# One-hots of the G build stored token by token in a hybrid SSM / attention / PEER kernel

## The chip, the cores and the metric

The kernel runs on one core of one Trainium2 chip. The metric is the device time of one execution in microseconds (us), the median of several runs. TensorE is PE in the rows (PEld is its weight load), VectorE is DVE, ScalarE is ACT, GpSimd is POOL, and SP issues DMAs.

## The reference

A residual stream of 512 tokens by 1024 runs through one Mamba-2 layer and one sliding-window attention layer, and behind each of them through a PEER feed-forward layer and a gated embedding. Only PEER matters here:

```python
q = (h @ q_w).reshape(T, PEER_HEADS, 2, PEER_HALF)
s = jnp.einsum('thcd,ckd->thck', q, sub_keys)            # 8 heads x 2 halves x 128 keys
s1, i1 = lax.top_k(s[:, :, 0], 16)
s2, i2 = lax.top_k(s[:, :, 1], 16)
cand_s = s1[..., :, None] + s2[..., None, :]             # 256 candidates per head
cand_i = i1[..., :, None] * 128 + i2[..., None, :]
best_s, best_pos = lax.top_k(cand_s, 16)
idx  = take_along_axis(cand_i, best_pos)                 # 8 x 16 experts of 16384 per token
gate = softmax(best_s)
a = einsum('nd,nhkd->nhk', h, u[idx]);  w = gate * gelu(a)
out = einsum('nhk,nhkd->nd', w, v[idx])
```

## The kernel before, in words

The 128 tokens of the first token tile (tt = 0) are done as the reference says: their 128 expert rows each are gathered by indirect DMA (lines 678 to 695). For the other 384 tokens (ND) the kernel computes all 16384 experts densely, in 128 blocks of 128 experts, and multiplies by a matrix G that holds the gate of each chosen expert and zero elsewhere.

The function `peer(L)` runs once for each of the two layers. Its first part makes queries, scores and the first top-k. Its u loop then runs over 128 blocks: each block is 24 float32r matmuls of 384 columns in `lin` / `mm3` (lines 202 to 204), the weights of which come by DMA, are split into a high and a low half on ScalarE (line 169) and GpSimd (line 172, four pieces), and the result goes through Gelu to DRAM (line 990). Beside it a generator `bg()` is advanced: `self.step(BRATE)` hands out 2.65 units of credit per block, and each item of its list has a cost (6.0 a top-k, 5.0 half a decode, 1.5 a one-hot batch). Beside that again, 1.17 gathers per block run (`gather(URATE)`). The v loop follows with 24 matmuls per block and no G work.

The G items are what the change touches. One item is a batch of QT = 4 tokens; there are 96 a layer, 192 in all. For a batch, `onehot(b)` on VectorE makes two tiles of 1024 fp16 elements per partition (a partition is one of the 128 head-and-rank slots): `o` (line 880; its tile shares the name "early" with score tiles), which compares the numbers 0 to 127 (`iota`) with both halves of the expert index (`iT`), and `og` (line 882), which multiplies the first half's one-hot by the gate's high and low fp16 part (`gT`). One item later `gmm(b, o)` issues 8 fp16 matmuls of 128x128 by 128 columns (line 895, for each of 4 tokens two that add up in one PSUM bank), and ScalarE copies the bank out (line 896) into a tile from which G goes to DRAM. A group of 8 such matmuls is called a burst below. The one-hot of the next item is made while a burst runs: `o` has three buffers, `og` two, so VectorE waits at line 882 when it is two bursts ahead.

In memory the token is the innermost dimension before: `o` is [2 halves, 128 numbers, 4 tokens], so that the four tokens of one number lie side by side, VectorE reads the indices of four tokens as a run of four fp16, and a matmul reads one token's one-hot with a step of 4 elements (8 bytes):

```python
mm(ps[:, q * P:(q + 1) * P], o[0][:, 1, :, q], o[1][:, j, :, q], start=(j == 0), stop=(j == 1))
```

`o[0][:, 1, :, q]` is the stationary operand (weight load), `o[1][:, j, :, q]` the moving one. `iT` and `gT` are filled in `decode_e`'s `turn` from a PSUM transpose (lines 868 to 870), three times a layer. The decode (lines 831 to 838) also reads the first 16 entries of `iota`, each four times side by side.

Of the kernel before, what the change touches and what calls it, by code (L numbers as in the profile page):

```python
# [16 lines left out]
AF = _mybir.ActivationFunctionType  # L17
OP = _mybir.AluOpType
AX = _mybir.AxisListType

P = 128
# [5 lines left out]
TOPK = 16  # L27
NBLK = 128
NG = P
ND = NT - NG  # L30
# [4 lines left out]
QT = 4  # L35
GSCALE = 32768.0
F16 = _mybir.dt.float16
# [11 lines left out]
C_ID, C_TRI, C_ROT, C_IOTA, C_I16, C_INV = 0, 128, 256, 384, 512, 528  # L49
# [13 lines left out]
class Net:  # L63
# [54 lines left out]
    def plan(self):  # L118
        t, s = self.t, self.srcs
        w, off = t["wlin"], 0  # L120

        def lin(n):
            nonlocal off
            for _ in range(n):
                s.append(w[off])
                off += 1

        def peer(i):
            lin(16)
            for j in range(NBLK):  # L130
                s.append(t["ut"][i * NBLK + j])
            for j in range(NBLK):
                s.append(t["v"][i * NBLK + j])

        lin(66)
        peer(0)
        lin(8 + 21)
        peer(1)
        lin(8)
# [500 lines left out]
    def peer(self, L):  # L640
        nc, t, tc = self.nc, self.t, self.tc
        mm = nc.tensor.matmul
        vt = nc.vector
# [103 lines left out]
        with ExitStack() as ctx:  # L747
            mp = ctx.enter_context(tc.tile_pool(name="pm", bufs=2, reuse_waits="tile"))
            hp = ctx.enter_context(tc.tile_pool(name="ph", bufs=1, reuse_waits="tile"))
# [24 lines left out]
            early = {}  # L774
            best = hp.tile([P, NTT, HEADS, TOPK], F32, name="best")
            pos = hp.tile([P, NTT, HEADS, TOPK], U32, name="pos")
            idx = hp.tile([P, 2, NTT, HEADS, TOPK], U32, name="idx")
            iT = hp.tile([P, 2, ND], F16, name="iT")
            gT = hp.tile([P, 2, ND], F16, name="gT")
            iota = hp.tile([P, P, QT], F16, name="iota")  # L780
            vt.tensor_copy(iota, self.const[:, C_IOTA:C_IOTA + P, None].to_broadcast([P, P, QT]))

            def top16(items):
                for f in (lambda x, v, i: vt.max(v[:, 0:8], x),
# [23 lines left out]
            HK = HEADS * TOPK  # L808
            dec = {}

            def fl(ap):
                return ap.rearrange("p a b -> p (a b)")
# [7 lines left out]
            def decode_i(tt, c):  # L820
                pi = mp.tile([P, HEADS, TOPK], U32, name="pi", bufs=1)
                if c == 0:
                    vt.tensor_single_scalar(pi, pos[:, tt], 4, op=OP.logical_shift_right)
                else:
                    vt.tensor_single_scalar(pi, pos[:, tt], 15, op=OP.bitwise_and)
                pb = mp.tile([P, TOPK, HEADS], F16, name="pb", bufs=1)
                vt.tensor_copy(pb, pi.rearrange("p h k -> p k h"))
                ib = mp.tile([P, TOPK, HEADS], F16, name="ib")
                vt.tensor_copy(ib, idx[:, c, tt].rearrange("p h a -> p a h"))
                eq = mp.tile([P, TOPK, HK], F16, name="eq", bufs=1)  # L830
                vt.tensor_tensor(eq.rearrange("p a (n q) -> p a n q", q=QT),  # L831
                                 fl(pb).rearrange("p (n q) -> p n q", q=QT)[:, None].to_broadcast([P, TOPK, HK // QT, QT]),
                                 iota[:, :TOPK, None, :].to_broadcast([P, TOPK, HK // QT, QT]), op=OP.is_equal)
                e4 = eq.rearrange("p a (k h) -> p a k h", h=HEADS)
                vt.tensor_tensor(e4, e4, ib[:, :, None, :].to_broadcast([P, TOPK, TOPK, HEADS]), op=OP.mult)  # L835
                n = TOPK // 2
                while n > 1:
                    vt.tensor_tensor(eq[:, :n], eq[:, :n], eq[:, n:2 * n], op=OP.add)  # L838
                    n //= 2
                f = mp.tile([P, HK], F32, name=f"fi{c}", bufs=1)  # L840
                vt.tensor_tensor(f, eq[:, 0], eq[:, 1], op=OP.add)
                dec[tt][1].append(f)

            def decode_e(tt):
                gt, fi = dec.pop(tt)
                sm = mp.tile([P, 2, HEADS], F32, name="sm")
                vt.tensor_reduce(sm[:, 0], gt, axis=AX.X, op=OP.add)
                vt.reciprocal(sm[:, 1], sm[:, 0])
                gk = mp.tile([P, TOPK, HEADS], F32, name="gk", bufs=1)
                vt.tensor_tensor(gk, gt.rearrange("p h k -> p k h"), sm[:, 1, None, :].to_broadcast([P, TOPK, HEADS]),  # L850
                                 op=OP.mult)
                if tt == 0:
                    ef = wg[:, 0]
                    vt.tensor_scalar(ef, fi[0], float(P), float(L * NBLK * P), op0=OP.mult, op1=OP.add)
                    vt.tensor_tensor(ef, ef, fi[1], op=OP.add)
                    vt.tensor_copy(eg, ef)
                    vt.tensor_copy(gate, fl(gk))

                def turn():
                    if tt == 0:  # L860
                        self.gi = 0
                        return
                    pt = self.bank(7)
                    for j, src in enumerate(fi + [fl(gk)]):
                        nc.tensor.transpose(pt[:, j * P:(j + 1) * P], src, self.ident)
                    ts = slice(tt * P - NG, (tt + 1) * P - NG)
                    for j in range(2):
                        nc.scalar.activation(iT[:, j, ts], pt[:, j * P:(j + 1) * P], AF.Copy)
                    nc.scalar.activation(gT[:, 0, ts], pt[:, 2 * P:3 * P], AF.Copy, scale=GSCALE)
                    vt.scalar_tensor_tensor(gT[:, 1, ts], pt[:, 2 * P:3 * P], GSCALE, gT[:, 0, ts], op0=OP.mult,  # L870
                                            op1=OP.subtract)
                return turn

            gs = {}

            def onehot(b):
                o = mp.tile([P, 2, P, QT], F16, name="early", bufs=3)
                og = mp.tile([P, 2, P, QT], F16, name="og")
                ts = slice(QT * b - NG, QT * b - NG + QT)
                vt.tensor_tensor(o, iota[:, None].to_broadcast([P, 2, P, QT]),  # L880
                                 iT[:, :, None, ts].to_broadcast([P, 2, P, QT]), op=OP.is_equal)
                vt.tensor_tensor(og, o[:, 0:1].to_broadcast([P, 2, P, QT]), gT[:, :, None, ts].to_broadcast([P, 2, P, QT]),  # L882
                                 op=OP.mult)
                return o, og

            def gmm(b, o):
                b -= NG // 4
                if b % GQ == 0:
                    i = b // GQ % 2
                    gs[b // GQ] = gsz[0][:, 4 * i:4 * i + 4].rearrange("p a b -> p (a b)").rearrange("p (a t) -> p a t", t=GT)  # L890
                x = gs[b // GQ]
                ps = gb()
                for q in range(4):
                    for j in range(2):
                        mm(ps[:, q * P:(q + 1) * P], o[0][:, 1, :, q], o[1][:, j, :, q], start=(j == 0), stop=(j == 1))  # L895
                nc.scalar.activation(x.rearrange("p a t -> p t a")[:, 4 * (b % GQ):4 * (b % GQ) + 4, :],
                                     ps.rearrange("p (q a) -> p q a", q=4), AF.Copy, scale=1.0 / GSCALE)
                if b % GQ == GQ - 1:
                    nc.scalar.dma_start(G[b // GQ], x.rearrange("p a t -> p (a t)"))
# [9 lines left out]
            def bg():  # L909
# [6 lines left out]
                def D(tt):  # L916
                    items.append((0.3, lambda: decode_g(tt), 2))
                    items.append((5.0, lambda: decode_i(tt, 0)))
                    items.append((5.0, lambda: decode_i(tt, 1)))
                    items.append((0.8, lambda: decode_e(tt), 2))  # L920

                def G_(tt, lo, hi):
                    def one(b):
                        o = onehot(b)
                        return lambda: gmm(b, o)
                    for b in range(32 * tt + lo, 32 * tt + hi):
                        items.append((1.5, lambda b=b: one(b)))
# [24 lines left out]
            for c in range(2 * HEADS):  # L952
                if c < 2:
                    ps = pair[c]
                else:
                    ps = mmb()
# [5 lines left out]
                q = hp.tile([P, NT], F32, name="ga", bufs=3)  # L962
# [16 lines left out]
            for j in range(NBLK):  # L979
                ps = mmb()  # L980
# [22 lines left out]
        with vctx:  # L1003
            mp = vctx.enter_context(tc.tile_pool(name="pv", bufs=3, reuse_waits="tile"))
# [549 lines left out]
```

## Time and profile before

| | us |
|---|---|
| median of 3 runs | 3490.18 (3489.79 to 3500.37) |
| the profiled execution | 3494.42 |
| its span in the trace | 3492.6 |
| u loop with G items, layer 0 | about 700 to 1210 |
| u loop with G items, layer 1 | about 2280 to 2793 |

TensorE is busy in 97% of the span, VectorE in 76%, GpSimd in 56%, ScalarE in 42%. Matmuls are pipelined and their recorded durations overlap, so how much time one takes is read from the distance between two starts, not from its duration. [...]

### The profile page before, as it was taken

The page shows a single profiled execution, that of the slowest core. Times are in us where ns is not written, and L with a number is a line of the kernel's source. Part 1 is how long each engine was busy: PE and PEld are TensorE (multiplying, and loading weights), DVE is VectorE, ACT ScalarE, POOL GpSimd, SP SyncE. Part 2 cuts the span into 40 slices and gives each one's busy share as a digit, 9 for nine tenths or more (in the row PEclk, how much of TensorE's full clock was granted, in tenths as well). Part 3 has the DMA queues.
Part 4 walks back from the last instruction along what each step waited for, and adds up shares of the span by engine and source line. Part 5 has one row for each costly group of instructions (what it writes and reads, how often), then busy time and mean ns, then how long its engine had stood idle before and what let it go on. Part 6 is the DMA issues. An engine that isn't in the chain of part 4 may idle for free.

```text
span 3492.6 us, 52247 instructions
## 1 busy us (share of the span) xinstructions
PE 3374.0 (97%) x18814; PEld 3109.2 (89%) x18814; DVE 2647.7 (76%) x4878; ACT 1454.1 (42%) x2198; POOL 1941.5 (56%) x2168
## 2 busy tenths in 40 slices
PE   8999999999999999999998999999999999999997
PEld 6777777999999989999996668999999999999996
DVE  7666677898888637887777956899888637877775
ACT  4443333444445533333334553444445533333334
POOL 5445445788887882322216235788888784222214
PEclk9999999999999999999999999999999999999998
DMA  3222222588888889999983122488888889999982
GB/s 119 89 72 73 73 67 69 166 295 283 312 303 288 309 292 365 349 341 347 338 281 107 43 67 87 148 274 299 299 317 281 301 309 357 349 342 336 341 306 85
DMA packets 357300, 827.50 MB, mean 237 GB/s; under 512 B 30000, under 2 KB 196528, under 8 KB 350896
## 3 DMA queue, kind: packets, MB, share of 16 engines
q1 hardware_dynamic: 235136, 448.59, 39.2%
q0 software_dynamic: 73728, 268.47, 21.3%
q10 hardware_dynamic: 48176, 107.10, 8.0%
q8 instruction: 147, 2.41, 0.3%
q14 instruction: 113, 0.93, 0.1%
HBM read 717.09 MB, written 106.95 MB: 236 GB/s over the span
## 4 chain that ended last, share of the span: by engine, by line
PE 70%; DVE 18%; POOL 5%; DMA 3%; issue 3%; ACT 1%; SPq 0%; POOLq 0%; ACTq 0%; DVEq 0%
PE bank L202 20%; PE bank L203 20%; PE bank L204 20%; PE bank L895 4%; POOL wlo L172 3%; DVE row L678 2%; DMA row<-u,eg 2%; DVE eq L838 1%; DVE og L882 1%; DVE early L880 1%; POOL row L695 1%; PE bank L968 1%; DVE eq L835 1%; PE bank L542 1%; DVE eq L831 1%
## 5 line engine op out<-in xcount | busy, mean ns | idle before, releaser
L172 POOL TENSOR_TENSOR wlo<-wraw,whi 128x256 fp32r<-128x256 f32 x1564 | 1262.3, 839 | 601.0 <-ACT whi L169 553.0
L169 ACT ACTIVATE whi<-wraw 128x1024 fp32r<-128x1024 f32 x647 | 685.3, 1061 | 760.3 <-issue 303.5
L204 PE MATMUL bank<-hhi,wlo 128*128 128x384 f32 x2048 | 697.2, 340 | 14.0 <-POOL wlo L172 13.9
L202 PE MATMUL bank<-hhi,whi 128*128 128x384 f32 x2048 | 707.8, 346 | 0.4 <-ACT whi L169 0.4
L695 POOL DMA_INDIRECT row<-v,eg x256 | 294.2, 1149 | 733.5 <-DVE yg L687 719.0
L203 PE MATMUL bank<-hlo,whi 128*128 128x384 f32 x2048 | 695.7, 340 | 0.0
L203 PE MATMUL bank<-vlo,whi 128*128 128x384 f32 x2032 | 684.2, 337 | 6.4 <-DVE vlo L744 6.4
L202 PE MATMUL bank<-vhi,whi 128*128 128x384 f32 x2032 | 684.8, 337 | 0.8 <-ACT vhi L742 0.8
L204 PE MATMUL bank<-vhi,wlo 128*128 128x384 f32 x2032 | 683.7, 336 | 0.0
L172 DVE TENSOR_TENSOR wlo<-wraw,whi 128x1024 fp32r<-128x1024 f32 x256 | 313.1, 1223 | 148.6 <-ACT whi L169 147.3
L204 PEld LDWEIGHTS bank<-hhi,wlo 128*128 128x128 f32 x2048 | 387.4, 189 | 19.8 <-POOL wlo L172 19.4
L202 PEld LDWEIGHTS bank<-hhi,whi 128*128 128x128 f32 x2048 | 390.2, 191 | 0.8 <-ACT whi L169 0.8
L203 PEld LDWEIGHTS bank<-vlo,whi 128*128 128x128 f32 x2032 | 382.6, 188 | 8.2 <-DVE vlo L744 8.2
L203 PEld LDWEIGHTS bank<-hlo,whi 128*128 128x128 f32 x2048 | 388.9, 190 | 0.0
L202 PEld LDWEIGHTS bank<-vhi,whi 128*128 128x128 f32 x2032 | 382.7, 188 | 2.0 <-ACT vhi L742 1.5
L204 PEld LDWEIGHTS bank<-vhi,wlo 128*128 128x128 f32 x2032 | 382.6, 188 | 0.1
L678 DVE SCALAR_TENSOR_TENSOR row<-row,pair 128x1024 f32<-128x1024 f32 x256 | 305.5, 1211 | 96.1 <-DMA row<-u,eg 96.1
L687 DVE SCALAR_TENSOR_TENSOR yg<-row,wg,yg 128x1024 f32<-128x1024 f32 x254 | 327.9, 1291 | 38.0 <-DMA row<-v,eg 38.0
L202 PE MATMUL bank<-z,whi 128*128 128x512 f32 x728 | 320.2, 440 | 3.4 <-DVE sg L1134 3.4
L990 ACT ACTIVATE ga<-bank 128x384 f32<-128x384 f32 x256 | 125.6, 491 | 471.1 <-PE bank L204 470.8
L695 POOL DMA_INDIRECT row<-u,eg x256 | 276.1, 1079 | 49.6 <-issue 23.4
L203 PE MATMUL bank<-z,whi 128*128 128x512 f32 x728 | 291.1, 400 | 4.7 <-DVE z L262 4.7
(321 smaller groups left out, 4995.9 us busy)
## 6 DMA issues: line engine op xcount, KB each, us to landing
wraw<-ut SPq DMA_DIRECT2D x256, 512.0 KB, 4.5
wraw<-v SPq DMA_DIRECT2D x256, 512.0 KB, 6.1
wraw<-wlin SPq DMA_DIRECT2D x135, 512.0 KB, 3.4
GA<-ga ACTq DMA_DIRECT2D x256, 192.0 KB, 4.2
G<-gsz ACTq DMA_DIRECT2D x48, 1024.0 KB, 7.0
gv<-G SPq DMA_DIRECT2D x96, 512.0 KB, 9.5
gsz<-GA SPq DMA_DIRECT2D x256, 192.0 KB, 6.8
PJ<-nf ACTq DMA_DIRECT2D x16, 256.0 KB, 2.0
```

The lines of the kernel that those rows point to most:

```text
L169: nc.scalar.activation(hi, r, AF.Copy)
L172: self.lo_eng.tensor_tensor(lo[:, q:q + n], r[:, q:q + n], hi.bitcast(F32)[:, q:q + n], op=OP.subtract)
L202: mm(out, whi, xhi, start=start, stop=False)
L203: mm(out, whi, xlo, start=False, stop=False)
L204: mm(out, wlo, xhi, start=False, stop=stop)
L542: mm(o[r * 64:(r + 1) * 64], X[:, (2 * q + r) * 64:(2 * q + r + 1) * 64], M[:, 2 * q + r, :], start=(c == 0), stop=True, skip_group_check= ...
L678: vt.scalar_tensor_tensor(r, r, 1.0, self.pair, op0=OP.mult, op1=OP.mult, accum_out=wg[:, 0, j:j + 1])
L687: vt.scalar_tensor_tensor(yg, r, wg[:, 0, j:j + 1], yg, op0=OP.mult, op1=OP.add)
L695: nc.gpsimd.indirect_dma_start(out=got[i], out_offset=None, in_=t["u"] if i < NJ else t["v"].rearrange("a p d -> (a p) d"), in_offset=bass ...
L831: vt.tensor_tensor(eq.rearrange("p a (n q) -> p a n q", q=QT), fl(pb).rearrange("p (n q) -> p n q", q=QT)[:, None].to_broadcast([P, TOPK, ...
L895: mm(ps[:, q * P:(q + 1) * P], o[0][:, 1, :, q], o[1][:, j, :, q], start=(j == 0), stop=(j == 1))
L990: nc.scalar.activation(ga[:, NG:], ps[:, NG:], AF.Gelu)
```

## The change

The tiles of the one-hots become [4 tokens, 2 halves, 128 numbers]: each token's 128 fp16 lie side by side, for the weight load as for the moving operand. The index and gate tiles get a last dimension of 2 that holds the same value twice, so that VectorE's operand, which is now the same for all 128 numbers of a token and half, is read as a pair of equal fp16, 64 times over. `iota` is no longer stored four times; a small tile `i16` takes its place in the decode.

```diff
-            iT = hp.tile([P, 2, ND], F16, name="iT")
-            gT = hp.tile([P, 2, ND], F16, name="gT")
-            iota = hp.tile([P, P, QT], F16, name="iota")
-            vt.tensor_copy(iota, self.const[:, C_IOTA:C_IOTA + P, None].to_broadcast([P, P, QT]))
+            iT = hp.tile([P, ND, 2, 2], F16, name="iT")
+            gT = hp.tile([P, ND, 2, 2], F16, name="gT")
+            iota = hp.tile([P, P], F16, name="iota")
+            vt.tensor_copy(iota, self.const[:, C_IOTA:C_IOTA + P])
+            i16 = hp.tile([P, TOPK, QT], F16, name="i16")
+            vt.tensor_copy(i16, self.const[:, C_I16:C_I16 + TOPK, None].to_broadcast([P, TOPK, QT]))
...
-                                 iota[:, :TOPK, None, :].to_broadcast([P, TOPK, HK // QT, QT]), op=OP.is_equal)
+                                 i16[:, :, None, :].to_broadcast([P, TOPK, HK // QT, QT]), op=OP.is_equal)
...
+                    two = lambda j: pt[:, j * P:(j + 1) * P, None].to_broadcast([P, P, 2])
                     for j in range(2):
-                        nc.scalar.activation(iT[:, j, ts], pt[:, j * P:(j + 1) * P], AF.Copy)
-                    nc.scalar.activation(gT[:, 0, ts], pt[:, 2 * P:3 * P], AF.Copy, scale=GSCALE)
-                    vt.scalar_tensor_tensor(gT[:, 1, ts], pt[:, 2 * P:3 * P], GSCALE, gT[:, 0, ts], op0=OP.mult,
-                                            op1=OP.subtract)
+                        nc.scalar.activation(iT[:, ts, j], two(j), AF.Copy)
+                    nc.scalar.activation(gT[:, ts, 0], two(2), AF.Copy, scale=GSCALE)
+                    vt.scalar_tensor_tensor(gT[:, ts, 1], two(2), GSCALE, gT[:, ts, 0], op0=OP.mult, op1=OP.subtract)
...
-                o = mp.tile([P, 2, P, QT], F16, name="early", bufs=3)
-                og = mp.tile([P, 2, P, QT], F16, name="og")
+                o = mp.tile([P, QT, 2, P], F16, name="early", bufs=3)
+                og = mp.tile([P, QT, 2, P], F16, name="og")
                 ts = slice(QT * b - NG, QT * b - NG + QT)
-                vt.tensor_tensor(o, iota[:, None].to_broadcast([P, 2, P, QT]),
-                                 iT[:, :, None, ts].to_broadcast([P, 2, P, QT]), op=OP.is_equal)
-                vt.tensor_tensor(og, o[:, 0:1].to_broadcast([P, 2, P, QT]), gT[:, :, None, ts].to_broadcast([P, 2, P, QT]),
-                                 op=OP.mult)
+                pairs = lambda ap: ap.rearrange("p t c (a d) -> p t c a d", d=2)
+                alike = lambda ap: ap[:, ts, :, None, :].to_broadcast([P, QT, 2, P // 2, 2])
+                vt.tensor_tensor(pairs(o), iota.rearrange("p (a d) -> p a d", d=2)[:, None, None].to_broadcast(
+                    [P, QT, 2, P // 2, 2]), alike(iT), op=OP.is_equal)
+                vt.tensor_tensor(pairs(og), pairs(o)[:, :, 0:1].to_broadcast([P, QT, 2, P // 2, 2]), alike(gT), op=OP.mult)
...
-                        mm(ps[:, q * P:(q + 1) * P], o[0][:, 1, :, q], o[1][:, j, :, q], start=(j == 0), stop=(j == 1))
+                        mm(ps[:, q * P:(q + 1) * P], o[0][:, q, 1], o[1][:, q, j], start=(j == 0), stop=(j == 1))
```

No instruction is moved. On every engine the same instructions stand in the same order, except that VectorE gets one more cast at the start of each `peer`, ahead of the norm's short chain (`rst`). On VectorE there, before:

```order
L262 SCALAR_TENSOR_TENSOR z_125<-x_105,cols,z_124 128x512
L781 CAST iota<-const 128x512
L295 TENSOR_SCALAR rst<-bank_4768 128x4
L296 CAST rst<-rst 128x4
L297 TENSOR_SCALAR rst<-rst 128x4
```

And the same place now:

```order
L262 SCALAR_TENSOR_TENSOR z_125<-x_105,cols,z_124 128x512
L781 CAST iota<-const 128x128
L783 CAST i_4703<-const 128x64
L295 TENSOR_SCALAR rst<-bank_4770 128x4
L296 CAST rst<-rst 128x4
```

One cast of 512 elements has become one of 128 and one of 64; everything behind it stands as it stood.

## Rows read from the trace of the kernel before

**Rows 1.** The page: busy us of each engine (share of the span) and instructions.

```profile
PE 3374.0 (97%) x18814; PEld 3109.2 (89%) x18814; DVE 2647.7 (76%) x4878; ACT 1454.1 (42%) x2198; POOL 1941.5 (56%) x2168
```

**Rows 2.** Stretches, layer 0: length, busy us by engine (instructions), clock, DMA share, GB/s.

```profile
740.00:811.00 71.00, 70.39 (x442) 68.91 (x443) 63.77 (x116) 35.25 (x44) 57.70 (x67) 1.00 0.85 298
...
847.00:987.00 140.00, 136.38 (x833) 133.12 (x833) 117.20 (x244) 64.51 (x81) 119.88 (x137) 0.98 0.86 297
987.00:1069.00 82.00, 77.32 (x461) 75.78 (x459) 76.32 (x155) 38.06 (x49) 75.04 (x88) 0.99 0.86 303
1069.00:1171.00 102.00, 101.92 (x648) 99.09 (x648) 75.11 (x106) 54.20 (x64) 78.35 (x87) 0.98 0.82 288
```

**Rows 3.** The chain that ended last, layer 0: start us, us, what.

```profile
810.63 1.14 DVE row L678 x2
...
847.20 1.11 PE bank L895 x8
...
987.16 0.81 DVE og L882
...
1069.09 1.09 PE bank L895 x8
...
1173.22 0.95 POOL row L695
```

**Rows 4.** Timeline of TensorE at two bursts: start us, us, instruction, count.

```profile
869.90 0.34 PE L204 MATMUL bank<-hhi,wlo 128*128 128x384 f32 x1
870.08 2.05 PE L895 MATMUL bank<-og,early 128*128 128x128 f16 x16
...
872.15 0.34 PE L203 MATMUL bank<-hlo,whi 128*128 128x384 f32 x1
```

**Rows 5.** Line 895 alone in two single microseconds (PE, PEld, clock, DMA, GB/s).

```profile
1069.00:1070.00 1.00, 0.92 (x8) 0.80 (x7) 0.50 0.81 246
870.00:871.00 1.00, 0.92 (x8) 0.92 (x9) 1.00 1.00 422
```

**Rows 6.** Timeline of TensorE: float32r matmuls of 384 columns, then of 512.

```profile
2255.26 0.34 PE L202 MATMUL bank<-hhi,whi 128*128 128x384 f32 x1
...
2260.03 0.34 PE L202 MATMUL bank<-hhi,whi 128*128 128x384 f32 x1
...
1859.64 0.39 PE L202 MATMUL bank<-x,whi 128*128 128x512 f32 x1
...
1865.13 0.39 PE L202 MATMUL bank<-x,whi 128*128 128x512 f32 x1
```

**Rows 7.** Line 895 alone by stretch, layer 0 (PE, PEld, clock, DMA, GB/s).

```profile
740.00:811.00 71.00, 16.69 (x128) 13.76 (x128) 1.00 0.85 298
847.00:987.00 140.00, 27.71 (x209) 22.14 (x209) 0.98 0.86 297
1069.00:1171.00 102.00, 31.01 (x240) 26.00 (x240) 0.98 0.82 288
```

**Rows 8.** VectorE's longest waits in 740 to 811, 847 to 987, 1069 to 1171.

```profile
DVE og L882 <- PE bank L895: 5.6, 4, 3.4
...
DVE og L882 <- PE bank L895: 9.1, 4, 3.2
...
DVE og L882 <- PE bank L895: 21.6, 11, 3.4
```

**Rows 9.** Operations of one line: duration ns min/median/max, first and last start, forms.

```profile
L880 DVE TENSOR_TENSOR early<-iota,iT x192: 676/838/3562, 727.2 to 2779.4; 128x1024 f16<-128x1024 f16 x192
L882 DVE TENSOR_TENSOR og<-early,gT x192: 691/694/3525, 728.4 to 2782.1; 128x1024 f16<-128x1024 f16 x192
L1344 DVE TENSOR_TENSOR s<-s,asm x16: 1224/1224/1226, 1948.7 to 2053.8; 128x1024 f32<-128x1024 f32 x16
L868 ACT ACTIVATE iT<-bank x12: 272/274/277, 707.3 to 2645.7; 128x128 f16<-128x128 f32 x12
L781 DVE CAST iota<-const x2: 1515/1530/1544, 531.4 to 2112.8; 128x512 f16<-128x512 f32 x2
```

## Prediction

> **What bounds the kernel now.** I read the page first: TensorE is busy 97% of the span, VectorE 76% [rows 1]. A mean over stages with different limits says little, so I cut the u loop of layer 0 into stretches where the chain of waits changes hands [rows 2, 3]. The chain lies on TensorE up to 810, on VectorE from 810.63 to 847, on TensorE from 847.20 to 987, on VectorE from 987.16 to 1069, on TensorE from 1069.09 to 1171, and after that on GpSimd, which issues gathers and splits weights. The bursts of line 895 therefore matter in three stretches: 740 to 811, 847 to 987, 1069 to 1171. There TensorE is busy 71, 136 and 102 of 71, 140 and 102 us, and VectorE 64, 117 and 75. Layer 1 has the same six stretches at 2320 to 2870, and I count it as layer 0 again.
>
> How fast are the bursts? Sixteen fp16 matmuls start at 870.08, one float32r matmul of 384 columns follows, and the next starts at 872.15 [rows 4]. A 384-column matmul takes (2260.03 - 2255.26) / 27 = 0.177 us from start to start [rows 6], which leaves 2.07 - 0.177 = 1.89 us for sixteen, or 0.118 us for each. A 512-column matmul takes (1865.13 - 1859.64) / 24 = 0.229 us [rows 6], so 128 more columns cost 0.052 us, and by the same line a matmul of 128 columns would take 0.177 - 2 x 0.052 = 0.073 us. The fp16 matmuls, with half the bytes in each element, are 0.045 us slower than this. What they alone have is operands read in steps of 8 bytes.
>
> A second row says that the array's clock isn't their limit. The burst at 1069.09 ran at a granted clock of 0.50 (1.2 GHz) and its eight matmuls took 1.09 us [rows 3, 5]; the eight at 847.20 took 1.11 us [rows 3], and the stretch around 870 was at 1.00 (2.4 GHz) [rows 5]. A matmul limited by its 128 columns would have doubled. So something outside the array sets 0.118 us: reading the moving operand, reading the weights, or the hand-over from weight load to matmul. The first two become contiguous, the third stays.
>
> **The change part by part.** *The matmuls.* 1536 of them go from 0.118 us to a time that no row shows. The near bound is the line of the contiguous float32r matmuls, 0.073 us; the floor is that line without its fixed part, 0.052 us; the other end is 0.118 us, if the hand-over sets it, and a loss has no mechanism here, since each operand touches fewer bytes. I take 0.073, because the rows behind it are also a weight load of 128 columns before each matmul. That is 8 x 0.045 = 0.36 us a burst.
>
> [...] Rows 4 and 6 speak for a limit of reading, but cannot tell it from the hand-over; this is the second rival.
>
> *Where it lands.* In 740 to 811 there are 128 / 8 = 16 bursts, in 847 to 987 some 26, in 1069 to 1171 30 [rows 7]: 5.8, 9.4 and 10.8 us. TensorE cannot run ahead of VectorE, which makes the next one-hots; VectorE's reserve is the time that it waits at line 882 for a burst to free its buffer: 5.6, 9.1 and 21.6 us [rows 8]. So 5.6, 9.1 and 10.8 us pass, together 25.5. The mean clock of 0.98 in two stretches [rows 2] means some 10 us at 0.50, in which about three bursts run and 128 columns need about twice the time, so 1 us less: 24.5. In the two VectorE stretches and after 1171 a faster burst only waits longer: nothing. Two layers: 49 us.
>
> *What is late next.* In 1069 to 1171 GpSimd has 78 us of work and the DMA queues a share of 0.82 [rows 2]; in 91 us instead of 102 these become 0.86 and 0.92. In 847 to 987 GpSimd has 120 us of work [rows 2], 0.92 of the shortened 131 us. Both hold, and the gathers after 1171 then begin earlier, but with no more than a tenth to spare.
>
> *VectorE's one-hots.* The same two instructions a batch, 1024 elements each, the output contiguous before and after; the shortest took 676 and 691 ns [rows 9], which for 1024 elements is the packed rate (line 1344, unpacked float32 of as many elements, takes 1224 ns [rows 9]). The medians and the 3.5 us maxima above that come with the neighbours, and don't change. New is that one operand is a pair of fp16, 4 bytes, read 64 times, where it was a run of four. Bounds: 676 ns if pairs are enough for the packed rate, 1224 ns if not. Line 1344 also reads one 4-byte word again and again (its second operand is one number per 256 elements) at no extra cost, so re-reading a word is cheap; I take 676 ns, no change.
>
> *Small parts.* Eighteen copies on ScalarE (12 of iT, 6 of gT) and six operations on VectorE now write 256 elements instead of 128. Each costs between nothing and another 0.27 us, the time of line 868 now [rows 9]: at most 5 us in all on ScalarE, which is busy 42% [rows 1], at three places a layer, ahead of the one-hots that read them. The cast of 1.53 us [rows 9] becomes two shorter ones, at most 3 us less over both layers, where VectorE waits for scores soon after. The decode reads i16 as it read iota. I count these at nothing; if their cover were gone, they would be worth 3 us either way.
>
> The sum is 3494.4 (the profiled execution, 3492.6 of it span) less 49, 3445; against the median of the runs shown, 3490, it is **3441 us**.
>
> **The rivals.** *First: part of the gain only.* The fixed part of a matmul behind a weight load is larger for this form, say halfway, 0.096 us, or GpSimd and DMA, at 0.9 of their time, give half of it back. Either way half of 49: 3466 us. For it: the margins above, and that no fp16 burst with contiguous operands is in the trace. Against it: the float32r stream has the same weight load and its line is straight.
>
> *Second: no change.* The step of 8 bytes was never the limit, 0.118 us is the hand-over, and the time stays at 3490. For it: 0.118 us at both clocks fits a fixed latency as well as a read. Against it: 0.177 us for a 384-column matmul with the same hand-over leaves a fixed part of 0.177 - 3 x 0.052 = 0.021 us.
>
> *Third: slower.* The engine does not take pairs at the packed rate, and line 880 goes from 676 to 1224 ns, line 882 from 691 to 1224, 1.08 us a batch. VectorE's work with its waits for other things then sets the stretch: 71 - 5.6 + 16 x 1.08 = 83 instead of 71, 140 - 9.1 + 26 x 1.08 = 159 instead of 140, 102 - 21.6 + 30 x 1.08 = 113 instead of 102: 42 us a layer, 3574 us, with the batches in the two VectorE stretches not yet counted. A dearer re-read at half this price, 0.54 us a batch, costs 3 and 5 us in the first two and gives back 5 in the last: even, and a little slower with the VectorE stretches. So it decides from about 0.5 us a batch. For it: no row has an operand whose run is two fp16. Against it: line 1344's word, and that the run of four ran packed.
>
> [...]
>
> **How the numbers follow.** Forecast 0.58 (3441); first rival 0.17 (3466); second 0.12 (3490); third 0.13 (3500 to 3574). The floor of 0.052 us would give 0.53 us a burst: 5.6, 9.1 and 15.8 us, 30.5 less 1 a layer, so 3490 - 59 = 3431, and with a little of VectorE's reserve more, 3424. The range of 8 in 10 goes from 3424 to 3488: it takes in the forecast, the first rival and the near half of the second, and leaves out the third. A measurement of this kernel can tell about 0.3%, 10 us, from no change. Faster: 0.58 + 0.17 = 0.75; the same: 0.12; slower: 0.13.
>
> **What would show it.** In the trace after, sixteen matmuls of line 895's successor between two float32r matmuls should take 1.2 us instead of 1.9, and a burst at the 0.50 clock should now be slower than one at 1.00. The two one-hot operations should keep minima of 676 and 691 ns. VectorE's waits for bursts should shrink from 36 us a layer to about 15, and the last stretch should begin some 25 us earlier in layer 0 with its length unchanged. It would be wrong if the sixteen still take 1.9 us (second rival), if the minima are near 1224 ns (third), or if the bursts are fast and the last stretch grows by as much (first).

## The result, and the profile after

The changed kernel took 3455.14 us (median of 4 runs, 3450.98 to 3458.85), the kernel before 3495.27 us on the same chip (4 runs): a ratio of 0.9884, 95% interval 0.9871 to 0.9897. The profiled executions took 3453.39 and 3494.42 us, 41.0 us apart. That is faster by more than the 0.3% that a measurement can tell, and 8 us of the 49 forecast did not come.

The page gives the busy time of each engine, with its share of the span and its instructions; it answers [rows 1].

```profile
PE 3291.1 (95%) x18814; PEld 3022.6 (88%) x18814; DVE 2672.6 (77%) x4880; ACT 1455.2 (42%) x2198; POOL 1953.3 (57%) x2168
```

TensorE lost 83 us of work, twice the gain in time: the other half is new idle time. VectorE's work *grew* by 25 us, with only two instructions more.

**The burst.** TensorE's timeline of the kernel after (start, us, instruction, count) answers [rows 4]; line 898 is 895 of before:

```profile
866.14 1.03 PE L898 MATMUL bank<-og,early 128*128 128x128 f16 x8 [3.09 <-DVE og L886]
...
886.36 0.34 PE L204 MATMUL bank<-hhi,wlo 128*128 128x384 f32 x1
886.54 1.07 PE L898 MATMUL bank<-og,early 128*128 128x128 f16 x16
887.42 0.42 PE L202 MATMUL bank<-hhi,whi 128*128 128x384 f32 x1
887.68 0.34 PE L203 MATMUL bank<-hlo,whi 128*128 128x384 f32 x1
```

From the start of the sixteen to that of line 203 it is 887.68 - 886.54 = 1.14 us. Less one 384-column matmul (0.177 us) that leaves 0.963 us for sixteen, 0.060 us each, where it was 0.118. The burst at 866.14, after 3.09 us in which TensorE waited, took 1.03 us for eight, nearly as long as sixteen take at 886.54. The windows of these two places have the granted clock, a share of full speed, in the third column from the right:

```profile
866.00:867.00 1.00, 0.86 (x9) 0.86 (x9) 0.90 (x3) 0.00 (x0) 0.11 (x1) 0.50 0.98 393
...
886.00:888.00 2.00, 2.00 (x24) 1.84 (x23) 0.80 (x2) 0.81 (x2) 1.69 (x3) 1.00 0.72 212
```

Before, eight took 1.09 us at 0.50 and about as long at 1.00 [rows 3, 5]. Now eight take nearly as long at 0.50 as sixteen at 1.00: the clock has become their limit.

**The loop.** To compare the same work I cut the u loop at its blocks: 21 to 108, with all 96 bursts, and the rest of it. The views give the length, then busy us (instructions) of TensorE, its weight loads, VectorE, ScalarE and GpSimd, the granted clock, the DMA share and GB/s. Before: layer 0, the rest of its loop, layer 1:

```profile
727.70:1210.30 482.60, 468.94 (x2880) 457.75 (x2881) 405.86 (x736) 234.66 (x290) 405.81 (x462) 0.98 0.85 297
1210.30:1301.20 90.90, 84.50 (x466) 81.44 (x465) 30.72 (x38) 30.60 (x42) 79.06 (x94) 0.98 0.88 303
2310.90:2791.50 480.60, 469.19 (x2880) 458.01 (x2881) 408.30 (x735) 234.71 (x292) 406.04 (x460) 0.99 0.85 297
```

After, the same three:

```profile
730.40:1193.50 463.10, 428.19 (x2882) 415.78 (x2883) 426.01 (x734) 235.30 (x291) 402.64 (x460) 0.97 0.88 308
1193.50:1279.60 86.10, 82.40 (x466) 78.97 (x463) 30.01 (x40) 30.86 (x42) 75.87 (x93) 1.00 0.91 316
2291.10:2752.10 461.00, 427.99 (x2883) 416.01 (x2884) 413.33 (x735) 235.28 (x291) 404.86 (x460) 0.97 0.88 310
```

The gain is 19.5 us in layer 0 and 19.6 in layer 1, where 24.5 were forecast. The rest of layer 0's loop brought 4.8 more, and its bursts begin 2.7 us later than before. TensorE is busy 40.8 and 41.2 us less, and its idle time rose from 13.7 to 34.9 and from 11.4 to 33.0. So half of what the bursts save returns as waiting. For whom, the waits of TensorE say (line, waited for: us, times, longest). Over the whole run, before:

```profile
PE bank L895 <- DVE og L882: 26.3, 15, 3.4
```

and after:

```profile
PE bank L898 <- DVE og L886: 63.3, 35, 3.7
```

It waits 37 us more for one-hots. In the cut of layer 1 alone, before and after:

```profile
PE bank L895 <- DVE og L882: 12.7, 7, 3.3
...
PE bank L898 <- DVE og L886: 29.9, 16, 3.7
```

VectorE's waits of after in the same two cuts, layer 0 above and layer 1 below, answer [rows 8]:

```profile
DVE og L886 <- PE bank L898: 19.3, 15, 3.4
...
DVE og L886 <- PE bank L898: 20.6, 16, 2.0
```

Before these were 49.6 and 49.2 us: VectorE's reserve went down by 30 and 29 us a layer and is not used up.

**What holds the one-hots.** The durations of the two operations (ns min/median/max) answer [rows 9]: minima of 676 and 691 ns as before, so the pair operand is read as fast as the run of four was, and maxima of 3.5 us as before.

```profile
L884 DVE TENSOR_TENSOR early<-iota,iT x192: 676/798/3574, 728.7 to 2742.9; 128x1024 f16<-128x1024 f16 x192
L886 DVE TENSOR_TENSOR og<-early,gT x192: 691/694/3519, 729.8 to 2744.2; 128x1024 f16<-128x1024 f16 x192
```

The timeline of the kernel after shows one such maximum; these are the rows of VectorE and GpSimd that start from 857.6 to 862:

```profile
857.60 3.50 DVE L884 TENSOR_TENSOR early<-iota,iT 128x1024 f16<-128x1024 f16 x1
857.73 2.81 POOL L172 TENSOR_TENSOR wlo<-wraw,whi 128x256 fp32r<-128x256 f32 x4
...
860.70 1.23 POOL L695 DMA_INDIRECT row<-u,eg  x1 [0.16 <-issue]
...
861.21 0.69 DVE L886 TENSOR_TENSOR og<-early,gT 128x1024 f16<-128x1024 f16 x1
...
861.82 1.21 DVE L678 SCALAR_TENSOR_TENSOR row<-row,pair 128x1024 f32<-128x1024 f32 x1
...
861.95 2.11 POOL L172 TENSOR_TENSOR wlo<-wraw,whi 128x256 fp32r<-128x256 f32 x3
```

The one-hot at 857.60 begins 0.13 us before GpSimd's four pieces of line 172 and ends, at 861.10, 0.56 us after the last of them, at 860.54. These 0.13 and 0.56 us make the 0.69 us that such an operation takes alone; the 2.81 us of the pieces come on top. In this trace 38 of the 384 one-hot operations take over 2 us, and every one of them ends 0.55 to 0.56 us after the end of a GpSimd piece; all 179 that take over 0.8 us overlap with such pieces. The one at 861.21, beside the issue of a gather, takes 0.69 us. The chain that ended last (start, us, what) now passes through such operations in 740 to 811, where before it lay on TensorE:

```profile
764.17 3.41 DVE early L884
...
790.27 3.41 DVE early L884
```

### The profile page after: what moved, and what is told of

It reads as the page before. It is cut to its first block, busy times and chain, and to the rows that moved or that the text cites. A ratio compares the mean times of both kernels' runs of the same rounds, so it can differ in the third digit from the quotient of the medians.

```text
span 3451.6 us, 52253 instructions
## 1 busy us (share of the span) xinstructions
PE 3291.1 (95%) x18814; PEld 3022.6 (88%) x18814; DVE 2672.6 (77%) x4880; ACT 1455.2 (42%) x2198; POOL 1953.3 (57%) x2168
## 4 chain that ended last, share of the span: by engine, by line
PE 58%; DVE 25%; POOL 7%; issue 5%; DMA 4%; ACT 1%; SPq 0%; POOLq 0%; DVEq 0%; ACTq 0%
PE bank L202 17%; PE bank L203 17%; PE bank L204 17%; POOL wlo L172 6%; DVE row L678 4%; DVE early L884 3%; DVE og L886 2%; DMA row<-u,eg 2%; POOL row L695 2%; DVE eq L840 1%; PE bank L898 1%; DMA wraw<-ut 1%; PE bank L971 1%; DVE eq L833 1%; DVE eq L837 1%
## 5 line engine op out<-in xcount | busy, mean ns | idle before, releaser
L695 POOL DMA_INDIRECT row<-v,eg x256 | 310.0, 1211 | 716.8 <-DVE yg L687 700.2
L172 DVE TENSOR_TENSOR wlo<-wraw,whi 128x1024 fp32r<-128x1024 f32 x256 | 313.3, 1224 | 148.6 <-ACT whi L169 147.5
```

Source lines behind the costliest of these rows:

```text
L172: self.lo_eng.tensor_tensor(lo[:, q:q + n], r[:, q:q + n], hi.bitcast(F32)[:, q:q + n], op=OP.subtract)
L695: nc.gpsimd.indirect_dma_start(out=got[i], out_offset=None, in_=t["u"] if i < NJ else t["v"].rearrange("a p d -> (a p) d"), in_offset=bass ...
```

## The experiments

Theory A: the step of the moving operand sets the pace of the bursts, and no other part of the change matters. Its rivals were the stationary operand, the hand-over between weight load and matmul, and VectorE's pairs. Theory C, on the missing 8 us: VectorE is the next limit, and its one-hots are held by GpSimd's low halves. A kernel with a single run has one time and no interval.

### The matmuls alone

**mm_only**: the tiles and VectorE's operations of the kernel before; the matmuls read contiguous slices of them.

```diff
+                f0, f1 = (t.rearrange("p c a q -> p (c a q)") for t in o)
...
-    mm(ps[...], o[0][:, 1, :, q], o[1][:, j, :, q], ...)
+    mm(ps[...], f0[:, (2*q+1)*P:(2*q+2)*P], f1[:, (2*q+j)*P:(2*q+j+1)*P], ...)
```

> The one-hots are made as before (tokens innermost), and only the matmuls read 128 contiguous fp16 from the same tiles, so they read other numbers than they should and G is wrong; the time is that of the change's TensorE part alone. Theory A (the matmuls are the whole change, the pair operand of VectorE is free): the time of the changed kernel, 0.985 to 0.991 of before, sixteen matmuls in about 0.9 us. Theory B (the pair operand costs VectorE time that hid part of the gain): below 0.983.

3455.67 us, a ratio of 0.9888 (0.9866 to 0.9910): theory A's range, and the time of the whole change. What the matmuls read is all of the gain.

### VectorE's part alone

**dve_only**: the one-hots of the kernel after; the matmuls read the same bytes in steps of four elements.

```diff
-    mm(ps[...], o[0][:, q, 1], o[1][:, q, j], ...)
+    mm(ps[...], f0[:, 1, :, q], f1[:, j, :, q], ...)     # f0, f1: the tiles seen as [2, P, 4]
```

> The one-hots are made as in the changed kernel, and the matmuls read them in steps of 4 elements as before did (wrong numbers, so G is wrong). VectorE's part alone. Theory A: 0.997 to 1.003 of before, matmuls at 0.117 us each. Theory B: above 1.004, with longer durations of the two one-hot operations.

3490.4 us, 0.9987 (0.9975 to 0.9998). TensorE's timeline:

```profile
884.09 2.05 PE L899 MATMUL bank<-og,early 128*128 128x128 f16 x16
...
886.16 0.33 PE L203 MATMUL bank<-hlo,whi 128*128 128x384 f32 x1
```

The bursts are as slow as before, and the doubled indices, the pairs and the smaller iota together cost nothing that can be measured.

### Which operand

**weights_contig** and **moving_contig**: as mm_only, but only the first or only the second operand is contiguous.

```diff
 # weights_contig
-    mm(ps[...], o[0][:, 1, :, q], o[1][:, j, :, q], ...)
+    mm(ps[...], f0[:, (2*q+1)*P:(2*q+2)*P], o[1][:, j, :, q], ...)
 # moving_contig
+    mm(ps[...], o[0][:, 1, :, q], f1[:, (2*q+j)*P:(2*q+j+1)*P], ...)
```

> The kernel before, only the stationary operand read contiguously (wrong numbers, G is wrong), the moving one in steps of 4 elements. If reading the moving operand sets the pace: still 0.117 us a matmul, weight load down from 117 to about 97 ns. If the weight load sets it: 0.056 us a matmul.

> The kernel before, only the moving operand read contiguously (wrong numbers, G is wrong), the weights in steps of 4 elements. If reading the moving operand sets the pace: 0.056 to 0.07 us a matmul. If the weight load sets it: still 0.117 us. If each alone is enough to slow it down: 0.117 us here and with the weights contiguous.

3484.19 and 3456.74 us, a single run each. TensorE's timeline of weights_contig:

```profile
889.77 2.01 PE L896 MATMUL bank<-og,early 128*128 128x128 f16 x16
...
891.80 0.34 PE L203 MATMUL bank<-hlo,whi 128*128 128x384 f32 x1
```

and of moving_contig:

```profile
886.29 1.09 PE L896 MATMUL bank<-og,early 128*128 128x128 f16 x16
...
887.45 0.34 PE L203 MATMUL bank<-hlo,whi 128*128 128x384 f32 x1
```

By the same working that is 0.116 and 0.061 us a matmul. The moving operand sets the pace; the stationary one is worth 0.002 us, 3 us for all 1536 (an estimate from this burst). The weight load's own duration, which the expectation put at 97 ns in weights_contig, kept a median of 115 ns there.

### How the pace follows the step

**step2** and **step8**: the kernel after, both operands read in steps of two and of eight elements.

```diff
 # step2
+    mm(ps[...], f0[:, q//2, :, q%2], f1[:, q//2, :, j], ...)   # seen as [4, P, 2]
 # step8
+    mm(ps[...], f0[:, :, q], f1[:, :, 2*q+j], ...)             # seen as [P, 8]
```

> The changed kernel, its matmuls reading both operands in steps of 2 elements, 4 bytes (wrong numbers, G is wrong). If the moving operand is limited by the span of memory it crosses, half the span of step 4 should be near half the excess: 0.056 to 0.07 us a matmul. If any step costs the full price because fp16 neighbours are no longer taken together: 0.117 us, as with step 4.

> The changed kernel, its matmuls reading both operands in steps of 8 elements, 16 bytes (wrong numbers, G is wrong). Limited by the span crossed: about 0.23 us a matmul, twice step 4, and 3560 us or more. Limited by something that costs the same for every step: 0.117 us and about 3490 us.

3465.68 and 3697.16 us. TensorE's timeline of step2:

```profile
886.04 1.09 PE L899 MATMUL bank<-og,early 128*128 128x128 f16 x16
...
887.20 0.33 PE L203 MATMUL bank<-hlo,whi 128*128 128x384 f32 x1
```

and of step8:

```profile
882.47 3.96 PE L899 MATMUL bank<-og,early 128*128 128x128 f16 x16
...
886.44 0.33 PE L203 MATMUL bank<-hlo,whi 128*128 128x384 f32 x1
```

0.061 us at 4 bytes, 0.237 at 16; with 0.118 at 8 bytes and 0.060 at 2, the matmul keeps its pace at 4 bytes from element to element, takes twice as long at 8, and from 8 to 16 bytes its time doubles with the step. Both operands are stepped in these two runs; that the moving one sets the pace is shown at 8 bytes alone. A step of two elements gave nearly the whole gain in the burst.

### Is VectorE the next limit

**no_mult**: the kernel after without the second one-hot operation; the first one-hot serves as both operands.

```diff
-                og = mp.tile([P, QT, 2, P], F16, name="og")
-                vt.tensor_tensor(pairs(og), pairs(o)[:, :, 0:1]..., alike(gT), op=OP.mult)
-                return o, og
+                return o, o
```

> The changed kernel without the multiplication by the gates (the second one-hot operation, 0.97 us of VectorE 192 times); the matmuls use the first tile for both operands, so G holds no gates. Theory C (after the change VectorE sets the u loop, which took half of TensorE's gain): TensorE gets what it is owed, 3395 to 3425 us, its waits for one-hots below 40 us. Theory D (the gain was lost to GpSimd's splits, gathers and DMA, and VectorE is only late with them): 3440 us or more.

3378.7 us, below what either theory gave. Half of the one-hot work gone is worth 76 us, and TensorE waits 18.2 us for one-hots where it waited 63.3:

```profile
PE bank L896 <- DVE early L883: 18.2, 14, 2.1
```

So in the kernel after some four tenths of the VectorE work that is taken away (the 186 us of line 886) come out as time. The edit does one thing more: without og, VectorE has the three buffers of the first tile to run ahead with, not two. What that is worth isn't separated.

### Does GpSimd hold the one-hots

**no_split**: the kernel after without GpSimd's low halves in the u loop up to four blocks before its end.

```diff
-            lo = self.hl.tile([P, D], F32R, name="wlo")
+            lo = hi if self.alone else self.hl.tile([P, D], F32R, name="wlo")
...
-            for q in range(0, D, n):
+            for q in range(0, 0 if self.alone else D, n):
...
+                self.alone = j < NBLK - 4
```

> The changed kernel without GpSimd's low halves of the weights in the u loop: the matmuls take the high half twice, so the results are off. Theory C1 (VectorE is late because GpSimd's work holds its one-hot operations back): their means fall from 1.18 and 0.97 us to 0.70, none is above 2 us, and the time is 3390 to 3425 us. Theory C2 (VectorE has too much work by itself): the means stay near 1 us and the time at 3440 us or more.

3356.19 us, below what either theory gave; the means are those of theory C1. The durations of the two operations (its lines are one further down):

```profile
L885 DVE TENSOR_TENSOR early<-iota,iT x192: 676/686/690, 715.0 to 2642.6; 128x1024 f16<-128x1024 f16 x192
L887 DVE TENSOR_TENSOR og<-early,gT x192: 691/693/697, 715.7 to 2644.3; 128x1024 f16<-128x1024 f16 x192
```

Not one of 384 operations is held any more. The hold by GpSimd is shown. In the kernel after the means are 1185 and 971 ns, so it costs VectorE (1185 - 686 + 971 - 693) x 192 = 149 us, 75 a layer (an estimate from the means). The time gained is not the price of the hold alone, since GpSimd's own work went with it.

### A gap between the pieces

**gap**: the kernel after with a one-element memset on GpSimd between the second and the third piece, from block 14 of the u loop up to four blocks before its end.

```diff
+                if self.halve and q == n:
+                    nc.gpsimd.memset(self.dot, 0.0)
...
+                self.halve = 14 <= j < NBLK - 4
```

> The changed kernel with a one-element memset on GpSimd between the second and the third piece of each low half in the u loop. If a one-hot operation of VectorE gets in wherever GpSimd turns to something that reads no SBUF: none of them above 2.2 us, means down by 0.1 to 0.3 us, 3425 to 3450 us. If it waits until GpSimd's queue of pieces is empty: still some 30 above 2 us, and 3450 to 3470 us for the added work.

3453.66 us, 0.9874 (0.9848 to 0.9899): no change. Of the 384 one-hot operations 38 take over 2 us, as many as without the memset, and the longest 3.8 us. GpSimd's timeline shows how little the memset parts the pieces:

```profile
878.99 1.95 POOL L174 TENSOR_TENSOR wlo<-wraw,whi 128x256 fp32r<-128x256 f32 x2
880.89 0.09 POOL L176 MEMSET dot<- 128x1 f32 x1
880.94 2.28 POOL L174 TENSOR_TENSOR wlo<-wraw,whi 128x256 fp32r<-128x256 f32 x2
```

The memset begins before the second piece ends, at 880.94, and the third begins as the second ends. So this memset of 0.09 us between the pieces, which opens no pause, doesn't let VectorE in; whether a pause would isn't shown.

### Work that is handed out more slowly, and a deeper buffer

**spread**: credit per block 2.4 instead of 2.65. **deep**: three buffers for og instead of two. **spread_deep**: both.

```diff
-URATE, VRATE, BRATE = 1.17, 0.94, 2.65
+URATE, VRATE, BRATE = 1.17, 0.94, 2.4          # spread, spread_deep
...
-                og = mp.tile([P, QT, 2, P], F16, name="og")
+                og = mp.tile([P, QT, 2, P], F16, name="og", bufs=3)   # deep, spread_deep
```

> The changed kernel with 2.4 units of credit per block of the u loop instead of 2.65, so that top-k, decode and one-hots are spread over 120 blocks instead of 108. Theory C (VectorE's work in the first 108 blocks sets the time, the last 20 are free on VectorE): 0.990 to 0.997 of the changed kernel, 3420 to 3445 us. Theory D: 3455 us or slower, since the last blocks are set by GpSimd and DMA already.

> The changed kernel with three buffers for the second one-hot tile instead of two, so that VectorE can be three bursts ahead of TensorE. If the 40 us that VectorE still waits for bursts are what it lacks later: 3435 to 3450 us. If VectorE is behind in stretches where no buffer would have been free earlier: 3450 to 3460 us, no change.

> The changed kernel with both the 2.4 units of credit per block and the third buffer of the second one-hot tile. If the two help in different stretches: 0.978 to 0.981 of before, 3418 to 3430 us. If the buffer only matters where VectorE's work is packed as tightly as with 2.65: the same as with 2.4 alone, 0.981 to 0.984.

spread took 3433.49 us, 0.9822 (0.9806 to 0.9839), inside theory C's range. deep took 3446.34, 0.9875 (0.9856 to 0.9894), an interval that holds the 0.9884 of the change: it decides nothing. spread_deep took 3421.54 us, 0.9794 (0.9777 to 0.9811), the fastest of those that do the whole work, 34 us below the kernel after. VectorE's two operations in it (busy us, mean ns, idle before them and what ended it):

```profile
L884 DVE TENSOR_TENSOR early<-iota,iT 128x1024 f16<-128x1024 f16 x192 | 260.6, 1358 | 2.2 <-PE bank L898 2.2
L886 DVE TENSOR_TENSOR og<-early,gT 128x1024 f16<-128x1024 f16 x192 | 217.8, 1134 | 6.6
```

In the kernel after they are:

```profile
L884 DVE TENSOR_TENSOR early<-iota,iT 128x1024 f16<-128x1024 f16 x192 | 227.5, 1185 | 0.0
L886 DVE TENSOR_TENSOR og<-early,gT 128x1024 f16<-128x1024 f16 x192 | 186.4, 971 | 56.7 <-PE bank L898 39.9 <-issue 0.5
```

With both edits VectorE hardly waits for bursts any more: its idle time in front of line 886 falls from 56.7 us, of which 39.9 were such waits, to 6.6, and 2.2 us are new in front of line 884. But this is the third buffer's doing. In deep, which has that edit alone, the two operations are:

```profile
L884 DVE TENSOR_TENSOR early<-iota,iT 128x1024 f16<-128x1024 f16 x192 | 251.8, 1312 | 6.2 <-PE bank L898 6.2
L886 DVE TENSOR_TENSOR og<-early,gT 128x1024 f16<-128x1024 f16 x192 | 184.2, 959 | 6.6
```

The time of deep can't be told from that of the kernel after, and spread, which brings 22 of the 34 us, leaves 58.6 us of idle time in front of line 886. Part of what VectorE no longer waits goes into longer holds: the two operations together take 436.0 us in deep and 478.4 in spread_deep, where they take 413.9 in the kernel after. Whether the two edits would do the same for the kernel before wasn't tried.

## Why the prediction was right, and where its sizes were off

**The direction and the mechanism held.** The step of 8 bytes was the limit (moving_contig), it was the moving operand's, not the stationary one's, which the prediction had left open, and the gain lies in the u loops. The second rival is excluded: 0.060 us instead of 0.118, with the same hand-over. A step of 8 bytes on the moving operand alone took 0.116 us (weights_contig), nearly twice the time, and 16 bytes on both operands 0.237 us (step8), four times. The third rival is excluded by dve_only and by the minima of 676 and 691 ns. That reading one word again and again cost line 1344 nothing shows in the trace of before: line 172 on VectorE, which reads two whole float32 operands of 1024 elements, took a median of 1224 ns too. The argument from the clock held as well: contiguous bursts do slow down at the granted clock of 0.50, eight in 1.03 us where sixteen take 1.07 at 1.00. The traces give this clock as a share of full speed alone; the GHz that the prediction sets beside it stand in no run.

**The first term was taken too dear.** 0.073 us was the end of the float32r line; 0.060 us was measured, between it and the floor of 0.052. The prediction called that line straight, but it had two points, 384 and 512 columns, and two points can't show it. A burst saves 8 x 0.058 = 0.46 us instead of 0.36. With this price alone, and by the prediction's own caps, a layer would have gained 5.6 + 9.1 + 13.8 = 28.5 us before the clock, some 55 us in all with the 1 us that the prediction took off for it. Measured were 41. So it is partly luck that the forecast of 49 came as near as it did: a price that was too dear hid part of the fault of the next step.

**The step that failed is the cap.** It said that each stretch can use up all the time that VectorE waits at line 882. In the last of its three stretches it took 10.8 of 21.6 us, in the first two all. What happened to VectorE's reserve can be counted, since its work and its idle time make up the length of a cut. Layer 0: waits at line 886 fell by 57.6 - 27.9 = 29.7 us and waits for gathers by 15.5 - 6.1 = 9.4, together 39.1 (of all idle time, 76.7 to 37.1, 39.6), but VectorE's own work took 20.2 us longer, and 19.5 us is left. Layer 1: all idle time fell by 24.6 us, the work took 5.0 longer, and 19.6 is left. The prediction said of the one-hots' medians and maxima that they "come with the neighbours, and don't change". They didn't grow (medians of 798 and 694 ns after 838 and 694), but the work did: 38 operations take over 2 us where 28 did, and by their line groups in the cut the one-hots alone took 14 us longer in layer 0, and in layer 1 no longer than before.

```profile
L884 DVE TENSOR_TENSOR early<-iota,iT 128x1024 f16<-128x1024 f16 x95 | 117.7, 1239 | 0.0
L886 DVE TENSOR_TENSOR og<-early,gT 128x1024 f16<-128x1024 f16 x96 | 94.6, 985 | 27.9 <-PE bank L898 19.3 <-issue 0.5
```

These are layer 0's groups after. Before:

```profile
L880 DVE TENSOR_TENSOR early<-iota,iT 128x1024 f16<-128x1024 f16 x96 | 110.8, 1154 | 0.0
L882 DVE TENSOR_TENSOR og<-early,gT 128x1024 f16<-128x1024 f16 x96 | 87.4, 910 | 57.6 <-PE bank L895 49.6 <-DVE early L880 0.9
```

The other runs tell that this comes with the faster bursts, not with the way VectorE makes the one-hots. Over the whole run, one trace each, the two operations together take 398.6 us before, 403.3 in dve_only and 399.7 in weights_contig, where the moving operand is read in steps of 8 bytes; they take 413.9 after, 419.3 in mm_only, 417.3 in moving_contig and 426.7 in step2, where it is read in steps of 2 or 4. How much of it falls on which layer is, as I read it, a matter of which one-hots meet GpSimd's pieces; no run shows that by itself.

In layer 1, where the work hardly grew, the other half of the failure shows: VectorE waits 20.6 us for bursts in the cut while TensorE waits 29.9 us for one-hots, where it waited 12.7 before. The two wait in turn. My reading, which no single run isolates: a one-hot held for 3.5 us makes TensorE wait, the bursts that follow close up, and then VectorE stands with both buffers of og full. Reserve that lies in one place doesn't help in another, and it was added up as if it did. The third buffer takes VectorE's waits for bursts away (39.9 to 6.2 us in deep) and leaves TensorE 51.5 of its 63.3 us of waits for one-hots, with a gain that is within the noise. So those waits were no reserve that more room alone turns into time; 34 us came only when the work was handed out more slowly as well.

**The clock probably took more than 1 us a layer.** Behind a wait of 3.09 us the clock stood at 0.50 (the burst at 866.14); the mean clock of the span fell from 0.990 to 0.983, and the cuts stand at 0.97 after 0.98 and 0.99. 96 bursts at 0.46 us would be 44 us, and TensorE's busy time fell by 41, so that some 3 us a layer, by this estimate, were lost to the lower clock. This differs from run to run: mm_only took 3450.99 us at a mean clock of 0.989.

**The first rival.** It named GpSimd and DMA, at 0.9 of their time, as what gives part of the gain back. They did not do so by running out of time: GpSimd's work in the cuts is the same (402.6 after 405.8 us), and the stretch after the bursts did not grow; it became 4.8 us shorter, and began 16.8 us earlier (1193.5 after 1210.3) where the prediction had some 25. GpSimd does reach TensorE through VectorE, by the hold, and the holds grew. But the kernel before has holds too, and it wasn't run without them, so which part of the missing gain they took isn't shown.

**Small parts.** ScalarE's iT copies went from a median of 274 ns [rows 9] to a mean of 381, inside their bound of 0.27 us more, and mm_only, which doesn't have them, is as fast as the change. They cost nothing that can be measured.

**Open.** Which part of the 76 and 99 us of no_mult and no_split is the hold, and which the work left out; through which wait spread alone gains 22 us, as TensorE's waits for one-hots are 60.8 us in it, hardly less than 63.3; and how much of the shortfall the holds took.

## What to carry to other kernels

Look at the step of a matmul's moving operand: in this kernel 16-bit elements 2 and 4 bytes apart took the same time (0.060 and 0.061 us a matmul of 128 columns), 8 bytes twice (0.118) and 16 bytes four times that (0.237), and the stationary operand's step, at 8 bytes, hardly mattered (0.002 us), so when only one can be contiguous, these runs speak for the moving one. When an engine that is busy 97% becomes faster, count the waits of its supplier by place, not as a sum: two engines that wait in turn leave reserve on both sides. And when the supplier's durations have a maximum five times their minimum, find out what holds them before taking them as constant.

## What the runs showed of the hardware

- **At 8 and 16 bytes the time goes with the step.** With both operands stepped, 128 columns of fp16 took 0.060, 0.061, 0.118 and 0.237 us at steps of 2, 4, 8 and 16 bytes, so the last two go with the bytes crossed: 1024 in 0.118 us and 2048 in 0.237, about 8.7 bytes per ns in each partition (an estimate, worked out from these two). At 8 bytes it was the moving operand's step: 0.116 us where it alone was stepped, 0.061 where it alone was contiguous.
- **A short matmul with its weight load cost 0.060 us** in these bursts at a granted clock of 1.00, less than the float32r line of the trace before led to expect (0.073).
- **GpSimd held a VectorE operation through several of its instructions.** The one-hot at 857.60 began 0.13 us before GpSimd's pieces and still ended 0.56 us after the last of the four, 3.50 us in all; a one-element memset among the pieces, which opened no pause, changed nothing (38 one-hots over 2 us with it and without). Without the pieces no one-hot took more than 0.697 us. Line 678, which reads one of its two inputs from PSUM, took 1.21 us beside such pieces and never more than 1.22. Why the operation that started first was the one to wait for all four pieces, no run here shows.
